# Three attention mixers: the value product with the probabilities as the stationary side

## The chip, the cores and the metric

The program runs on one core of a Trainium2 chip. The metric is the device time of one execution in microseconds. Five engines work side by side in that core: TensorE (PE, with its weight loads shown apart as PEld), VectorE (DVE), ScalarE (ACT), GpSimd (POOL) and SyncE (SP, which here only starts transfers).

## What is computed

Two blocks of two layers each run on 256 tokens of width 1024. In the first block, layer 0 mixes by a differential attention and a gated recurrence, layer 1 by dilated attention with 16 heads of 64. In the second block each layer holds a gated linear attention of 4 heads, a neighbourhood attention of 6 heads and a sliding-window attention of 6 heads with a sink, all of head width 64; its layer 0 also carries a context of 256 tokens through its own attention. Feed-forward layers stand between them. The attention that the change touches is this, in the reference:

```python
# dilated attention (block 1, layer 1), one branch
m = jnp.max(s, axis=-1, keepdims=True)
e = jnp.exp(s - m)
den = jnp.sum(e, axis=-1)
o = jnp.einsum('bhrnqk,bhrnkd->bhrnqd', e.astype(v.dtype), vw) / den[..., None].astype(v.dtype)
...
# sliding window with a sink (block 2)
p = jax.nn.softmax(jnp.concatenate([s_loc, s_ctx, s_sink], axis=-1), axis=-1)
...
o = (jnp.einsum('bhgnqk,bnkhd->bnqhgd', p_loc, vb)
     + jnp.einsum('bhgnqk,blhd->bnqhgd', p_ctx, vc))
```

The neighbourhood attention is the same without the sink and with a bias; the context's attention has its own 256 keys alone.

## The kernel before

**The dense work.** All weights come from HBM in units of 512 KB or less (`WeightStream`, lines 195 to 223). SP starts the transfer into `wr`, ACT rounds it to `wh` (line 214), DVE takes the rest `wl` (line 216), and each product of activations and weights is made of three matmuls, `xh*wh`, `xh*wl`, `xl*wh`, on operands of type fp32r that pass the array once. These matmuls, 256 or 512 columns wide, are most of PE's work.

**The small work** of the mixers (scores, transposes, value products) is in plain fp32. A plain fp32 matmul runs as two instructions in the profile, a transpose as one.

**One attention step** handles two heads (`c` = 0, 1) and one tile of 128 queries (`t`). It is a pipeline of three functions, `one`, `two` and `three`; at place i of the program `one` of step i, `two` of step i-1 and `three` of step i-2 are written down. `one` makes the scores and the softmax: maximum, exponential (ACT, which also adds up the sums), reciprocal, and then a DVE multiplication of each row of probabilities by its reciprocal (lines 751 and 1257). `two` transposes the probabilities on PE, 128 by 128 at a time, and copies them to SBUF. `three` is the value product (lines 774 and 1286): the values of a head (128 keys by 64) are the stationary operand, the transposed probabilities (128 keys by 128 queries) move, and the two heads go to output rows 0 to 63 and 64 to 127 of one PSUM tile. So the array works as two halves of 64 columns, written `128*64` in the profile, and the output has the feature on the rows and the token along the columns, as the output projection wants it. `y["T"].put` then splits it into high and low part (ACT line 357, DVE line 358).

There are 52 such steps: 16 in the dilated attention (8 with one key tile, 8 with two), 12 in the context's attention (two key tiles) and 24 in the latent attention of the two layers of block 2 (four key tiles). With two heads, so many key tiles and two instructions each, a step has 4, 8 or 16 value-product instructions, 576 in all.

**What sets the order.** The program is a list of items (`weave`, `side_by_side`) in which attention steps are woven into projections or feed-forward parts. A scheduler then orders each engine's instructions by a simulated timeline, so that the order on an engine isn't that of the code. PSUM has four buffers with the tag `acc`, two `sc`, one `sm`, one `fil`. The modulation (line 958) is a side job: its matmuls work on a quarter of the array's columns (`128*32`), with a stationary `cT` of 32 columns per step of which two carry data.

## Time and profile before

| | us |
|---|---|
| median of 3 runs | 1947.28 |
| lowest, highest | 1944.61, 1950.41 |
| the profiled execution's own time | 1951.42 |
| its span, first to last instruction | 1949.5 |
| PE busy | 1859.0 |
| weight loads (PEld) busy | 1582.9 |
| DVE busy | 1230.2 |
| ACT busy | 1006.3 |
| mean granted clock of TensorE | 0.967 |

Busy time is the union of an engine's instructions. Matmuls overlap each other, so how long PE takes over a stretch is read from the distance between the starts of its instructions, not from the durations. The granted clock is a share of 2.4 GHz.

### The profile page before, as it was taken

How to read it: one execution, taken by the hardware profiler on the slowest of the kernel's cores; microseconds unless marked ns; L12 is line 12 of the kernel's file. 1: busy time of each engine (PE TensorE's matmuls, PEld its weight loads, DVE VectorE, ACT ScalarE, POOL GpSimd, SP SyncE). 2: the span in 40 equal slices, each digit the busy share in tenths (PEclk: the TensorE clock that was granted, in tenths of full speed). 3: DMA queues.
4: the chain of work that ended last, by engine and by line, in shares of the span. 5: the costliest groups of instructions: out<-in, count | busy, mean ns of one | idle time of the engine just before them, and what ended most of it. 6: DMA issues, size and time to landing. Idle time of an engine off the chain costs nothing. (4 is left out here: it accounts for less than half of the span.)

```text
span 1949.5 us, 32053 instructions
## 1 busy us (share of the span) xinstructions
PE 1859.0 (95%) x12481; PEld 1582.9 (81%) x12481; DVE 1230.2 (63%) x2325; ACT 1006.3 (52%) x1669; POOL 168.0 (9%) x230
## 2 busy tenths in 40 slices
PE   8989999997999799999899999999999999979997
PEld 6766889886886588887697999989999986659997
DVE  5565566665666566667667786676646767655554
ACT  6354556444555355555456664454646556434443
POOL 3111300003110200002100000000000001100000
PEclk9999999997998889999899999999999999989999
DMA  8755654545666544446552445555664455346563
GB/s 294 245 173 195 200 192 152 184 145 185 194 217 196 175 154 153 161 155 214 165 184 90 125 149 161 177 186 180 190 188 154 143 184 171 122 151 176 185 181 106
DMA packets 101539, 338.87 MB, mean 174 GB/s; under 512 B 12212, under 2 KB 13516, under 8 KB 101388
## 3 DMA queue, kind: packets, MB, share of 16 engines
q1 hardware_dynamic: 86124, 286.00, 46.0%
q0 software_dynamic: 15264, 50.84, 7.9%
q8 instruction: 98, 1.61, 0.3%
q14 instruction: 53, 0.43, 0.1%
HBM read 335.73 MB, written 1.05 MB: 173 GB/s over the span
## 5 line engine op out<-in xcount | busy, mean ns | idle before, releaser
L216 DVE TENSOR_TENSOR wl<-wr,wh 128x1024 fp32r<-128x1024 f32 (+3 forms) x562 | 644.1, 1148 | 409.5 <-ACT wh L214 406.7
L214 ACT CAST wh<-wr 128x1024 fp32r<-128x1024 f32 (+3 forms) x562 | 549.3, 980 | 620.5 <-PE acc L281 129.1
L280 PE MATMUL acc<-wl,mh 128*128 128x256 f32 (+3 forms) x400 | 131.7, 330 | 1.5 <-DVE wl L216 1.5
L279 PE MATMUL acc<-wh,mh 128*128 128x256 f32 (+3 forms) x400 | 131.8, 336 | 0.0
L281 PE MATMUL acc<-wh,ml 128*128 128x256 f32 (+3 forms) x400 | 131.8, 331 | 0.0
L279 PE MATMUL acc<-wh,xh 128*128 128x512 f32 (+3 forms) x304 | 119.9, 401 | 2.6 <-ACT xh L378 1.9
L280 PE MATMUL acc<-wl,xh 128*128 128x512 f32 (+3 forms) x304 | 118.8, 391 | 0.5 <-DVE wl L216 0.5
L281 PE MATMUL acc<-wh,xl 128*128 128x512 f32 (+3 forms) x304 | 118.2, 390 | 0.0
L956 POOL DMA_DIRECT2D fr<-in_w_mod_dram x90 | 48.9, 545 | 661.9 <-PE fil L958 547.8
L854 PE MATMUL acc<-wh,a 128*128 128x512 f32 x256 | 101.5, 400 | 0.0
L856 PE MATMUL acc<-wh,a 128*128 128x512 f32 x256 | 101.1, 396 | 0.0
L855 PE MATMUL acc<-wl,a 128*128 128x512 f32 x256 | 101.1, 395 | 0.0
L1474 PE MATMUL sc<-xh,wh 128*128 128x256 f32 x352 | 100.4, 286 | 0.5 <-ACT xh L378 0.5
L1475 PE MATMUL sc<-xl,wh 128*128 128x256 f32 x352 | 100.7, 286 | 0.0
L1476 PE MATMUL sc<-xh,wl 128*128 128x256 f32 x352 | 100.2, 285 | 0.0
L1475 PE MATMUL sc<-ml,wh 128*128 128x256 f32 x352 | 98.9, 281 | 0.0
L1476 PE MATMUL sc<-mh,wl 128*128 128x256 f32 x352 | 98.7, 280 | 0.0
L1474 PE MATMUL sc<-mh,wh 128*128 128x256 f32 x352 | 98.7, 280 | 0.0
L958 PE MATMUL fil<-fr,cT 128*32 128x256 f32 x720 | 65.9, 422 | 31.2 <-DMA fr<-in_w_mod_dram 30.7
L279 PEld LDWEIGHTS acc<-wh,mh 128*128 128x128 f32 x400 | 75.2, 189 | 12.4 <-issue 4.8
L829 PE MATMUL sc<-mh,wh 128*128 128x256 f32 x256 | 74.1, 291 | 9.3 <-ACT mh L378 9.3
L280 PEld LDWEIGHTS acc<-wl,mh 128*128 128x128 f32 x400 | 75.9, 190 | 8.0 <-DVE wl L216 1.9
(580 smaller groups left out, 4853.5 us busy)
## 6 DMA issues: line engine op xcount, KB each, us to landing
wr<-in_ffn_w_dram SPq DMA_DIRECT2D x128, 512.0 KB, 3.4
fr<-in_w_mod_dram POOLq DMA_DIRECT2D x90, 512.0 KB, 5.0
wr<-in_w_gate_dram SPq DMA_DIRECT2D x66, 512.0 KB, 3.7
wr<-in_w_up_dram SPq DMA_DIRECT2D x66, 512.0 KB, 4.1
wr<-in_w_down_dram SPq DMA_DIRECT2D x66, 512.0 KB, 3.6
wr<-in_w_in_dram SPq DMA_DIRECT2D x40, 384.0 KB, 3.4
wr<-in_ev_w_in_dram SPq DMA_DIRECT2D x28, 512.0 KB, 5.4
wr<-in_w_in_dram SPq DMA_DIRECT2D x28, 512.0 KB, 3.9
```

Source lines behind the costliest of these rows:

```text
L214: S.copy(hi, raw)
L216: V.tensor_tensor(lo, raw, hi, ALU.subtract)
L279: mm(o, xh[:, k, :], wh[:, kk, :], start=(u == 0 and kk == 0), stop=False)
L280: mm(o, xh[:, k, :], wl[:, kk, :], start=False, stop=False)
L281: mm(o, xl[:, k, :], wh[:, kk, :], start=False, stop=(u == nu - 1 and kk == 1))
L829: mm(o, wh[:, kk, bs], mh, start=(k == 0 and b % 2 == 0), stop=False, skip_group_check=True)
L854: mm(o, hh[:, b, ts_], wh[:, kk, :], start=(b == 0), stop=False)
L855: mm(o, hh[:, b, ts_], wl[:, kk, :], start=False, stop=False)
L856: mm(o, hl[:, b, ts_], wh[:, kk, :], start=False, stop=(b == 3))
L1474: mm(o, wh[:, kk, bs], mh, start=(k == 0 and b == 0), stop=False, skip_group_check=True)
L1475: mm(o, wh[:, kk, bs], ml, start=False, stop=False, skip_group_check=True)
L1476: mm(o, wl[:, kk, bs], mh, start=False, stop=(k == 7), skip_group_check=True)
```

## The change

The roles in the value product are exchanged: in `heads_out` the transposed probabilities are stationary (all 128 columns of the array) and the 64 columns of values move. The output has tokens on the rows. It is multiplied by the reciprocal sums on its way out of PSUM into `yt` (DVE, line 729), transposed on PE into the other part of the same PSUM tile, and then split as before. The multiplications of the probabilities in `one` are gone. In the sliding window's latent part the sink becomes the start value of the first maximum, so that its own maximum goes. The remaining edits make room: `cT` shrinks to overlapping windows of 32 columns, and two small tags have three buffers in place of four. The differential attention (`da1`, `da2`, `da_out`) stays as it is.

```diff
-    cT = T([P, KD, 32], F32, "cT")
+    cT = T([P, 2 * KD + 30], F32, "cT")
...
-        v = T([P, n], F32, tag + "a", 4)
+        v = T([P, n], F32, tag + "a", 3)
...
+    def heads_out(y, blk, t, rr, pvs):
+
+        o = PT("acc")
+        for c, pairs in enumerate(pvs):
+            for j, (p, v) in enumerate(pairs):
+                mm(o[:, 64 * c:64 * c + 64], p, v, start=(j == 0), stop=(j == len(pairs) - 1))
+        yt = T([P, 2, 64], F32, "yt", 2)
+        V.tensor_tensor(yt, o[:, 0:P].rearrange("p (c n) -> p c n", c=2), rr.unsqueeze(2).to_broadcast([P, 2, 64]), ALU.mult)
+        tr(o[:, P:2 * P], yt.rearrange("p c n -> p (c n)"))
+        y["T"].put(blk, 1, t, o[:, P:2 * P].unsqueeze(1))
...
-            s, rr = softmax_pair(ps, C("odd")[:, 256 - nk:256], nk)
-            for c in range(2):
-                V.tensor_scalar(s[:, c, 0:nk], s[:, c, 0:nk], rr[:, c:c + 1], None, ALU.mult)
-            return (s,)
+            return softmax_pair(ps, C("odd")[:, 256 - nk:256], nk)
...
-            o = PT("acc")
-            for j in range(t + 1):
-                for c in range(2):
-                    hs = slice((2 * hp + c) * 64, (2 * hp + c) * 64 + 64)
-                    mm(o[64 * c:64 * c + 64, 0:P], v[:, j, hs], pT[:, c, j, :], start=(j == 0), stop=(j == t))
-            y["T"].put(4 * half + hp, 1, t, o[:, 0:P].unsqueeze(1))
+            heads_out(y, 4 * half + hp, t, rr,
+                      [[(pT[:, c, j, :], v[:, j, (2 * hp + c) * 64:(2 * hp + c) * 64 + 64]) for j in range(t + 1)]
+                       for c in range(2)])
...
-                mm(ps[32 * g:32 * g + 32, 0:256], cT[:, k, :], raw[:, 256 * g:256 * g + 256],
+                mm(ps[32 * g:32 * g + 32, 0:256], cT[:, 2 * k:2 * k + 32], raw[:, 256 * g:256 * g + 256],
...
-                                           ALU.max, mx[:, 1, c:c + 1])
+                    V.tensor_tensor_reduce(s[c][:, 256:W], ps[c][:, 256:W], zero.to_broadcast([P, 256]), 1.0,
+                                           -3.0e38 if na else sink[:, c:c + 1], ALU.add, ALU.max, mx[:, 1, c:c + 1])
...
-            if not na:
+            if e.ctx and not na:
                 V.tensor_tensor(m, m, sink, ALU.max)
...
-            for c in range(2):
-                V.tensor_scalar(s[c], s[c], sm[:, 0, c:c + 1], None, ALU.mult)
-            return (s,)
+            return s, sm[:, 0, :]
...
+            heads_out(y, 2 + hp, t, rr, [[(pTs[c][:, j * P:(j + 1) * P], value(c, j)) for j in range(nkt)] for c in range(2)])
```

**What moves, place by place.** In the rows below a name stands as output<-moving,stationary, a number at its end is the buffer's, and a plain fp32 matmul is one row although it runs as two instructions. First PE at the last step of block 2's layer 0, in the middle of the context's feed-forward (lines 1553 to 1555). Before:

```order
L1554 MATMUL acc_11854<-xl_10495,wh_11702 128x256
L1555 MATMUL acc_11854<-xh_10494,wl_11704 128x256
L1286 MATMUL acc_11879<-fr_11676,sv_9892 64x128 x4
L1286 MATMUL acc_11879<-fr_11676,csv_4409 64x128 x4
L1553 MATMUL acc_11854<-xh_10494,wh_11708 128x256
L1554 MATMUL acc_11854<-xl_10495,wh_11708 128x256
```

The value product of both heads stands among the dense matmuls, 64 output rows by 128 columns each. Now, at the same step:

```order
L1554 MATMUL acc_11885<-xl_10526,wh_11733 128x256
L1555 MATMUL acc_11885<-xh_10525,wl_11735 128x256
L727 MATMUL acc_11910<-sv_9918,fr_11704 128x64 x2
L727 MATMUL acc_11910<-csv_4409,fr_11704 128x64 x2
L727 MATMUL acc_11910<-sv_9918,fr_11704 128x64 x2
L727 MATMUL acc_11910<-csv_4409,fr_11704 128x64 x2
L1553 MATMUL acc_11885<-xh_10525,wh_11739 128x256
L1554 MATMUL acc_11885<-xl_10526,wh_11739 128x256
```

The product is again eight matmuls in a row, with 128 output rows by 64 columns and the probabilities (`fr`) as stationary side; the transpose of `yt` stands 27 matmuls further on.

Next PE at the end of the dilated attention (block 1, layer 1; `a_1210` are the values, `t_...` the probabilities). Before:

```order
L279 MATMUL acc_6405<-wh_6247,xh_4768 128x512
L280 MATMUL acc_6405<-wl_6249,xh_4768 128x512
L774 MATMUL acc_6453<-t_1339_6437,a_1210_5914 64x128 x2
L281 MATMUL acc_6405<-wh_6247,xl_4769 128x512
L774 MATMUL acc_6458<-t_1342_6451,a_1210_5914 64x128 x4
L279 MATMUL acc_6404<-wh_6247,xh_4768 128x512
L280 MATMUL acc_6404<-wl_6249,xh_4768 128x512
L281 MATMUL acc_6404<-wh_6247,xl_4769 128x512
```

The two last value products stand close together among the dense matmuls, and there is no transpose after them. Now, for the same end of the stage:

```order
L727 MATMUL acc_6446<-a_1217_5917,t_1337_6397 128x64 x4
L177 MATMUL acc_6456<-ident_61,t_1347_6431 128x128 x4
L279 MATMUL acc_6413<-wh_6252,xh_4768 128x512
L280 MATMUL acc_6413<-wl_6254,xh_4768 128x512
L281 MATMUL acc_6413<-wh_6252,xl_4769 128x512
L963 MATMUL fil_6815<-fr_6888,cT_72 32x256 x3
L963 MATMUL fil_6815<-fr_6894,cT_72 32x256 x4
L727 MATMUL acc_6463<-a_1217_5917,t_1352_6444 128x64 x2
L177 MATMUL acc_6446<-ident_61,yt_6451 128x128
L177 MATMUL acc_6463<-ident_61,yt_6466 128x128
L279 MATMUL acc_6414<-wh_6252,xh_4768 128x512
L280 MATMUL acc_6414<-wl_6254,xh_4768 128x512
```

Between the second last product (acc_6463) and the transpose of its quotient only one other transpose stands; the product before it (acc_6446) has sixteen between, seven of them modulation (line 963).

Last DVE at that same end of the dilated attention. Before:

```order
L494 RECIPROCAL rs_6430<-sm__1336_6424 128x2
L751 TENSOR_SCALAR t_1334_6422<-t_1334_6422,rs_6430 128x256 x2
L216 TENSOR_TENSOR wl_6402<-wr_6398,wh_6400 128x1024
L216 TENSOR_TENSOR wl_6469<-wr_6465,wh_6467 128x1024
L358 TENSOR_TENSOR xl_4769<-acc_6439,xh_4768 128x128
L216 TENSOR_TENSOR wl_6487<-wr_6483,wh_6485 128x1024
L358 TENSOR_TENSOR xl_4769<-acc_6453,xh_4768 128x128
```

The probabilities are multiplied (line 751) right behind the reciprocal, and only the low parts of the finished outputs (line 358) follow the weight splits (line 216). Now:

```order
L494 RECIPROCAL rs_6439<-sm__1349_6433 128x2
L216 TENSOR_TENSOR wl_6485<-wr_6481,wh_6483 128x1024
L216 TENSOR_TENSOR wl_6503<-wr_6499,wh_6501 128x1024
L729 TENSOR_TENSOR yt_6451<-acc_6446,rs_6361 128x128
L729 TENSOR_TENSOR yt_6466<-acc_6463,rs_6390 128x128
L358 TENSOR_TENSOR xl_4769<-acc_6446,xh_4768 128x128
L358 TENSOR_TENSOR xl_4769<-acc_6463,xh_4768 128x128
L729 TENSOR_TENSOR yt_6476<-acc_6471,rs_6439 128x128
```

The two multiplications of the probabilities are gone, and the two divisions of the outputs (line 729) stand behind two weight splits and ahead of the low parts.

## Rows read from the trace of the kernel before

**Rows 1.** The page: busy time, and PE in 40 slices (tenths busy).

```profile
PE 1859.0 (95%) x12481; PEld 1582.9 (81%) x12481; DVE 1230.2 (63%) x2325; ACT 1006.3 (52%) x1669; POOL 168.0 (9%) x230
...
PE   8989999997999799999899999999999999979997
```

**Rows 2.** Busy time of each engine in the four attention stretches.

```profile
core 0: us, PE busy (x) PEld busy (x) DVE busy (x) ACT busy (x) POOL busy (x), PEclk, DMA share, GB/s
540.00:652.00 112.00, 107.53 (x823) 82.61 (x816) 67.81 (x267) 59.00 (x156) 10.65 (x20) 0.94 0.63 201
700.00:873.00 173.00, 173.00 (x1159) 148.48 (x1159) 118.68 (x211) 99.75 (x182) 2.01 (x2) 1.00 0.51 167
1005.00:1190.00 185.00, 179.61 (x1350) 156.45 (x1349) 138.89 (x342) 118.50 (x204) 6.70 (x12) 0.99 0.43 138
1600.00:1705.00 105.00, 98.30 (x804) 71.72 (x803) 71.90 (x237) 51.94 (x119) 15.02 (x26) 0.94 0.46 146
```

**Rows 3.** What PE waited for in the whole span: total, times, longest, us.

```profile
PE fil L958 <- DMA fr<-in_w_mod_dram: 30.7, 19, 7.5
...
PE sm L177 <- DVE t L1257: 3.8, 2, 2.5
```

**Rows 4.** PE in order of time, latent layer 0, around one value product.

```profile
start us, us, engine line op out<-in xcount [idle before <-releaser]
...
1184.57 0.28 PE L1555 MATMUL acc<-xh,wl 128*128 128x256 f32 x1
1184.78 0.66 PE L1286 MATMUL acc<-fr,sv 128*64 128x128 f32 x8
1185.27 0.61 PE L1286 MATMUL acc<-fr,csv 128*64 128x128 f32 x8
1185.81 0.39 PE L1553 MATMUL acc<-xh,wh 128*128 128x256 f32 x1
1186.03 0.28 PE L1554 MATMUL acc<-xl,wh 128*128 128x256 f32 x1
```

**Rows 5.** PE, the gated mixer's output products, full-array form.

```profile
1176.27 0.28 PE L1555 MATMUL fil<-xh,wl 128*128 128x256 f32 x1
1176.39 1.90 PE L1152 MATMUL acc<-a,t 128*128 128x64 f32 x16
1178.21 0.27 PE L1161 MATMUL acc<-cf,t 64*64 64x64 f32 x1
```

**Rows 6.** PE, transposes: a row of them, and two between 512-wide matmuls.

```profile
1091.13 0.60 PE L177 MATMUL acc<-ident,t 128*128 128x128 f32 x4
...
639.45 0.39 PE L281 MATMUL acc<-wh,xl 128*128 128x512 f32 x1
639.69 0.38 PE L177 MATMUL acc<-ident,t 128*128 128x128 f32 x2
639.82 0.48 PE L279 MATMUL acc<-wh,xh 128*128 128x512 f32 x1
640.13 0.40 PE L280 MATMUL acc<-wl,xh 128*128 128x512 f32 x1
```

**Rows 7.** DVE by line: busy us, mean ns, idle before.

```profile
L216 DVE TENSOR_TENSOR wl<-wr,wh 128x1024 fp32r<-128x1024 f32 (+3 forms) x562 | 644.1, 1148 | 409.5 <-ACT wh L214 406.7
...
L1257 DVE TENSOR_SCALAR t<-t,sm 128x512 f32<-128x512 f32 x48 | 21.1, 482 | 0.5
...
L751 DVE TENSOR_SCALAR t<-t,rs 128x128 f32<-128x128 f32 (+1 forms) x32 | 8.7, 313 | 0.5
...
L1257 DVE TENSOR_SCALAR t<-t,csm 128x256 f32<-128x256 f32 x24 | 7.4, 350 | 0.4
...
L1170 DVE TENSOR_TENSOR t<-acc,g4stb 128x128 f32<-128x128 f32 x8 | 2.0, 286 | 4.4 <-POOL g4stb L385 4.3
...
L1247 DVE TENSOR_TENSOR mx<-mx,sink__56_234 128x2 f32<-128x2 f32 x6 | 0.9, 155 | 0.0
```

More of the change, by code (lines that the diff above doesn't have):

```diff
@@ L193, in params @@
         V.tensor_copy(prm.rearrange("p a l k -> p (a l k)"), pt[:, 0:96])
-        S.activation(cT[:, :, 0:2].rearrange("p k s -> p s k"), pt[:, 96:112].rearrange("p (s k) -> p s k", s=2), AF.Silu)
+        S.activation(cT[:, 0:2 * KD].rearrange("p (k s) -> p s k", s=2), pt[:, 96:112].rearrange("p (s k) -> p s k", s=2), AF.Silu)
     def PR(name, l):
@@ L381, in rsqrt_eps @@
     def rsqrt_eps(ms, n, eps, tag="st"):
-        v = T([P, n], F32, tag + "a", 4)
+        v = T([P, n], F32, tag + "a", 3)
         V.tensor_scalar(v, ms, eps, None, ALU.add)
-        r = T([P, n], F32, tag + "b", 4)
+        r = T([P, n], F32, tag + "b", 3)
         nc.gpsimd.tensor_tensor(r, v, mhalf[:, 0:n], ALU.pow)
@@ L748, in one, with two @@
                 mm(ps[c][:, 0:nk], q[r, hp, t * P:(t + 1) * P], k[r, hp, 0:nk], start=True, stop=True)
-            s, rr = softmax_pair(ps, C("odd")[:, 256 - nk:256], nk)
-            for c in range(2):
-                V.tensor_scalar(s[:, c, 0:nk], s[:, c, 0:nk], rr[:, c:c + 1], None, ALU.mult)
-            return (s,)
-        def two(half, hp, t, s):
+            return softmax_pair(ps, C("odd")[:, 256 - nk:256], nk)
+        def two(half, hp, t, s, rr):
             nk = P * (t + 1)
@@ L765, in two, with three @@
                 S.copy(pT, p4)
-            return (pT,)
-        def three(half, hp, t, pT):
+            return pT, rr
+        def three(half, hp, t, pT, rr):
             v = st["v", half]
-            o = PT("acc")
-            for j in range(t + 1):
-                for c in range(2):
-                    hs = slice((2 * hp + c) * 64, (2 * hp + c) * 64 + 64)
-                    mm(o[64 * c:64 * c + 64, 0:P], v[:, j, hs], pT[:, c, j, :], start=(j == 0), stop=(j == t))
-            y["T"].put(4 * half + hp, 1, t, o[:, 0:P].unsqueeze(1))
+            heads_out(y, 4 * half + hp, t, rr,
+                      [[(pT[:, c, j, :], v[:, j, (2 * hp + c) * 64:(2 * hp + c) * 64 + 64]) for j in range(t + 1)]
+                       for c in range(2)])
         def group(half, j0, t_outer=()):
@@ L1239, in one @@
                 else:
-                    V.tensor_tensor_reduce(s[c][:, 256:W], ps[c][:, 256:W], zero.to_broadcast([P, 256]), 1.0, -3.0e38, ALU.add,
-                                           ALU.max, mx[:, 1, c:c + 1])
+                    V.tensor_tensor_reduce(s[c][:, 256:W], ps[c][:, 256:W], zero.to_broadcast([P, 256]), 1.0,
+                                           -3.0e38 if na else sink[:, c:c + 1], ALU.add, ALU.max, mx[:, 1, c:c + 1])
                     nb = nbt[0][:, c, t, :] if na else (C("causal") if t == 0 else C("swa"))
@@ L1255, in one, with two @@
             V.reciprocal(sm[:, 0, :], sm[:, 0, :])
-            for c in range(2):
-                V.tensor_scalar(s[c], s[c], sm[:, 0, c:c + 1], None, ALU.mult)
-            return (s,)
-        def two(hp, t, s):
+            return s, sm[:, 0, :]
+        def two(hp, t, s, rr):
             if e.ctx or hp < 3:
@@ L1273, in two, with three, value @@
                     V.tensor_copy(pTs[c], pt[:, 0:W])
-            return (pTs,)
-        def three(hp, t, pTs):
-            o = PT("acc")
-            for j in range(nkt):
+            return pTs, rr
+        def three(hp, t, pTs, rr):
+            def value(c, j):
                 src = e if j < 2 else ctxkv
-                for c in range(2):
-                    if hp < 3:
-                        vv = src.nv[:, j % 2, (2 * hp + c) * 64:(2 * hp + c + 1) * 64]
-                    else:
-                        kv = (2 * hp - 6 + c) // 3
-                        vv = src.sv[:, j % 2, kv * 64:(kv + 1) * 64]
-                    mm(o[64 * c:64 * c + 64, 0:P], vv, pTs[c][:, j * P:(j + 1) * P], start=(j == 0), stop=(j == nkt - 1))
-            y["T"].put(2 + hp, 1, t, o[:, 0:P].unsqueeze(1))
+                if hp < 3:
+                    return src.nv[:, j % 2, (2 * hp + c) * 64:(2 * hp + c + 1) * 64]
+                kv = (2 * hp - 6 + c) // 3
+                return src.sv[:, j % 2, kv * 64:(kv + 1) * 64]
+            heads_out(y, 2 + hp, t, rr, [[(pTs[c][:, j * P:(j + 1) * P], value(c, j)) for j in range(nkt)] for c in range(2)])
         return pipeline([(hp, t) for hp in hps for t in range(2)], one, two, three)
```

## The prediction

> **What bounds the kernel now.** I read the page first. PE is busy for 95% of the span, DVE for 63%, and in 33 of the 40 slices PE stands at nine tenths or more [rows 1]. Then I read the same by stretch, for the four in which the changed steps run: the dilated attention (540 to 652 us), the context's attention (700 to 873), and the latent attention of block 2's layer 0 (1005 to 1190) and layer 1 (1600 to 1705). PE is busy for 558 of these 575 us, DVE for 397 [rows 2]. Third, what PE waited for: its longest wait in total is for the modulation's weights, 30.7 us; for the multiplied probabilities it waited 3.8 us in all, in two places [rows 3]. So in these stretches the order of PE's instructions, taken one after the other, sets the pace, and DVE is hidden. Last I read PE in order of time around single products, from start to start, since a union of durations hides what an instruction really costs there.
>
> **The price of one product instruction.** In the old form 16 instructions start between 1184.78 and the next dense matmul at 1185.81; the first eight last 0.66 us to the end of the last, and with 0.27 us for one they start (0.66 - 0.27)/7 = 0.055 us apart [rows 4]. The new form is in the trace already: the gated mixer's output product has a full 128-column stationary side and 64 moving columns. Sixteen of them last 1.90 us, so they start (1.90 - 0.27)/15 = 0.109 us apart [rows 5]. Transposes, with 128 stationary and 128 moving columns, start (0.60 - 0.27)/3 = 0.110 us apart [rows 6]. Halving the moving columns changes nothing there, and halving the stationary ones halves the price: loading the stationary side sets it. The exchange doubles the stationary columns of each instruction, from 64 to 128. With 576 product instructions that is 576 x (0.109 - 0.055) = **+31.1 us**.
>
> The Trainium skill's TensorEngine Tiling (Array Packing), section Performance Considerations, advises the opposite of the change: where the moving side has 64 columns or fewer, swap the two sides and tile by columns, for up to 2x. By that alone the products' 31.7 us would become 63.4 us. The rows agree on the factor of two, but the advice leaves out the next term, which works against it.
>
> **What the half arrays cost at their borders.** Before the group the distance from the last dense start to the first product is 0.21 us (1184.57 to 1184.78), where dense matmuls of 256 columns stand 0.12 apart: +0.09. Behind it, 16 x 0.055 = 0.88 us of the 1.03 us up to the next dense start are the group's own: +0.15. The dense matmul after that stands 0.22 behind instead of 0.12: +0.10 [rows 4]. Together 0.34 us a visit, or 0.17 for each change of the array's tiling. The new form shows none on entering: 1176.27 to 1176.39 is the usual 0.12 [rows 5]. Along PE's whole order I count 467 changes of tiling before and 400 now; some 110 go with the products and some come back, because modulation (`128*32`) and scores (`64*128`) are cut up more often. 67 x 0.17 = **-11.4 us**. How the new form leaves for dense matmuls no row shows; the nearest are transposes, after which two dense matmuls follow with nothing lost (below), so I take nothing. The other end is 0.34 us for each of 52 steps, +17.7 us, if all of a visit's price returned.
>
> **The 52 transposes.** Two transposes between 512-wide matmuls: from 639.45 to 640.13 is 0.68 us with one dense matmul in between, and two dense distances of 0.23 would be 0.46, so 0.11 us each [rows 6]. 52 x 0.11 = **+5.7 us**.
>
> **DVE.** It loses 48 x 0.482 + 24 x 0.350 + 32 x 0.313 = 41.5 us of multiplications, and 12 maxima of 0.155 us, 1.9 us. It gains 52 divisions of 128 x 128 out of PSUM; the gated mixer's division is the same form, 0.286 us, so 14.9 us [rows 7]. Net 28.5 us less, beside PE and so worth only what PE waited for it. Of the 3.8 us for the probabilities I take 3 back [rows 3]: **-3 us**; bounds 0 and -7, if the other DVE waits of these stretches go too.
>
> **The new wait.** Each step now goes from PE to DVE and back to PE. The scheduler puts work between: in the latent step shown, 27 dense matmuls, some 3.5 us at 0.12 and 0.23; the median step has about 3 us. In seven of the 52 I count less than 1.3 us between, four of them in the dilated attention, the nearest having one transpose between. One round is a matmul's 0.27 us and a division's 0.286 us and what is ahead of it on DVE, in the worst case a weight split of 1.148 us [rows 7], so 0.6 to 1.7 us against a mean cover of 0.8. I take 0.4 us for seven: **+3 us**; bounds 0 and, with a split ahead in a dozen places, +12. Behind a waiting transpose stand dense matmuls on PE; behind a waiting division stand weight splits on DVE, which PE then needs.
>
> **Edits at nothing.** The memset of `cT` shrinks at the start, where PE waits for other things. The smaller `cT` gives the modulation the same 32 stationary columns. Two tags with three buffers instead of four: their tiles are a few columns and POOL, which fills them, is busy 9% [rows 1]; if that cover is gone one step of the norms comes late, under 1 us. The sink as a start value costs DVE at most the 0.155 us a step that it saves.
>
> **The sum.** 31.1 - 11.4 + 5.7 - 3 + 3 = 25.4 us. PE's own waits in these stretches, for modulation weights above all, end at a fixed time, so some added work falls into them: PE isn't busy for 17 of 575 us [rows 2], and I take 4 us of that. 21.4 us against the profiled execution: its span of 1949.5 us and 1.9 us around it, 1951.4, becomes 1973. That execution stands 4.1 us above the median of the runs shown, 1947.3, to which the forecast refers: 1947.3 + 21.4 = **1969 us**.
>
> **Rivals.**
> *The stationary load hides and the moving columns count (faster).* The queue would load the next 128 columns while others move, and an instruction of 64 moving columns would cost no more than one of 128 does now, 0.055 us. Then the +31.1 us fall away and 25.4 becomes -5.7 us, 1942; at half of 0.055 another 576 x 0.027 = 15.8 us go, 1926. It decides below 0.065 us an instruction. Against it: the same form at 0.109 us, with nothing ahead of it that it waits for [rows 5]. In the Trainium skill's TensorE: Matmul & The Clock Gate, section Back-to-back issue gap, the table gives 134 cycles for 128 columns and about 60 for 64 at 2.4 GHz, which by itself makes the exchange a gain; the same section says that the load counts too. Chance 0.05.
> *PE's waits and DVE take it in (no change).* If the stretches wait for the softmax chain rather than for PE, the 28.5 us taken from DVE shorten that chain and the added PE work falls into waits. All 17 us of idle PE would have to be used, and the 7 us of DVE waits gone: 28.4 - 17 - 7 = 4 us, 1952. For it: 15 of the 17 us lie where steps are dense on DVE. Against: the context's stretch has no idle PE at all, and much of the idle time elsewhere is the modulation's transfers [rows 2, 3]. Chance 0.09.
> *The round over DVE decides (much slower).* If a division always stood behind a split, and its transpose at the head of PE's queue, each step would lose up to 1.7 us less its cover. It decides where the round takes over 3 us; 26 steps at 1 us make 26 us, 1995. Against: the cover in the order, and that DVE has less to do. Chance 0.05.
> *The borders stay (slower still than forecast).* The new form might pay on leaving what the old one paid: +17.7, 1987. Chance 0.08.
>
> **How the numbers follow.** The forecast has 0.73. Its own range is 1958 to 1980, from the bounds of the small terms. Taken with the neighbours on either side, **1953 to 1985** leaves out the fast rival, most of the much slower one and part of the border. About 0.3%, 5.8 us, is what a measurement of this kernel can tell from no change. Faster by more than that: the first rival and a sliver of lucky order, 0.06. Within: the second, 0.09. Slower: 0.85.
>
> **What would show it.** Right: line 727 with 576 instructions of the form `128*128 128x64`, starting 0.109 us apart and entered at 0.12; 52 transposes of `yt`; DVE's busy time some 28 us lower; the four stretches longer, the two latent ones most (24 x 16 of the 576 instructions); dense matmuls following a product at once. Wrong: product instructions near 0.055 us apart; PE waiting for `yt` from DVE by more than 10 us; the stretches as long as before with PE idle less; or a change outside of the four stretches as large as in them.

## The result

The changed kernel takes 1977.13 us in the median (1973.19 to 1982.53, 4 runs), the kernel before in the same series 1948.85 (4 runs). The ratio is 1.0134, with a 95% interval of 1.0107 to 1.0161: some 26 us slower, where 1969 us and +21.4 had been forecast. The profiled execution took 1978.46 us, with a span of 1976.7.

The page of the profile after, which answers to [rows 1]:

```profile
PE 1891.9 (96%) x12533; PEld 1623.7 (82%) x12533; DVE 1199.8 (61%) x2261; ACT 1003.9 (51%) x1669; POOL 170.8 (9%) x230
```

PE has 32.9 us more, DVE 30.4 less. The value product in the latent step of layer 0, in order of time, answers to [rows 4]:

```profile
1202.09 0.28 PE L1555 MATMUL acc<-xh,wl 128*128 128x256 f32 x1
1202.21 0.56 PE L727 MATMUL acc<-sv,fr 128*128 128x64 f32 x4
1202.60 0.61 PE L727 MATMUL acc<-csv,fr 128*128 128x64 f32 x4
1203.05 0.61 PE L727 MATMUL acc<-sv,fr 128*128 128x64 f32 x4
1203.49 0.61 PE L727 MATMUL acc<-csv,fr 128*128 128x64 f32 x4
1203.91 0.36 PE L1553 MATMUL acc<-xh,wh 128*128 128x256 f32 x1
1204.12 0.28 PE L1554 MATMUL acc<-xl,wh 128*128 128x256 f32 x1
```

The group is entered at the usual 0.12 us, and its 16 instructions take 1203.91 - 1202.21 = 1.70 us up to the next dense start, 0.106 us each. The dense matmul behind it stands 0.21 away in place of 0.12, so leaving costs 0.09. One visit takes 1.79 us, where the old form with its borders took 0.09 + 1.03 + 0.10 = 1.22 [rows 4].

The transpose of the quotient between two 512-wide dense matmuls (it answers to [rows 6]), and the division on DVE in the latent steps with its count, shortest, median and longest time in ns (it answers to [rows 7]):

```profile
1207.34 0.39 PE L1581 MATMUL acc<-wh,c 128*128 128x512 f32 x1
1207.57 0.27 PE L177 MATMUL acc<-ident,yt 128*128 128x128 f32 x1
1207.60 0.47 PE L1579 MATMUL acc<-wh,c 128*128 128x512 f32 x1
1207.91 0.39 PE L1580 MATMUL acc<-wl,c 128*128 128x512 f32 x1
```

```profile
L729 DVE TENSOR_TENSOR yt<-acc,sm x24: 278/285/294, 1034.4 to 1729.1; 128x128 f32<-128x128 f32 x24
```

From the dense matmul ahead of the transpose to the next but one is 1207.91 - 1207.34 = 0.57 us; less two dense distances of 0.23 that leaves 0.11. What PE waited for in the changed kernel, total, times and longest in us (the form of [rows 3]):

```profile
PE sc L834 <- ACT mh L378: 1.0, 1, 1.0
...
PE acc L177 <- DVE yt L729: 0.3, 1, 0.3
```

The new wait, PE for the quotient, is 0.3 us in the whole execution; for the modulation's weights PE waited 35.4 us, in before 30.7 [rows 3].

**Where the 27.2 us of the span went.** The 562 weight splits (line 216) come in the same order in both traces, so the start of one of them, after less before, tells how far behind the changed kernel is there. Cut at the same splits, the stretches that differ are these; first before (columns as in [rows 2]), then after:

```profile
core 0: us, PE busy (x) PEld busy (x) DVE busy (x) ACT busy (x) POOL busy (x), PEclk, DMA share, GB/s
0.00:162.90 162.90, 148.70 (x843) 107.38 (x844) 94.63 (x233) 84.70 (x166) 34.92 (x65) 0.97 0.68 227
548.30:660.10 111.80, 107.33 (x790) 80.75 (x788) 67.62 (x250) 57.71 (x147) 9.86 (x19) 0.94 0.59 187
660.10:704.80 44.70, 29.44 (x160) 23.59 (x160) 25.89 (x42) 18.34 (x37) 14.49 (x17) 0.73 0.41 145
704.80:899.70 194.90, 194.90 (x1275) 166.14 (x1274) 129.82 (x222) 106.73 (x186) 2.09 (x2) 1.00 0.53 174
899.70:1255.80 356.10, 344.37 (x2374) 297.94 (x2373) 252.71 (x504) 199.81 (x324) 28.80 (x32) 0.98 0.49 154
1589.20:1754.00 164.80, 145.49 (x1062) 108.43 (x1062) 106.31 (x311) 77.36 (x163) 19.74 (x34) 0.91 0.47 151
```

```profile
0.00:171.40 171.40, 155.89 (x843) 112.51 (x844) 93.68 (x233) 83.93 (x166) 34.89 (x65) 0.91 0.65 218
556.90:678.10 121.20, 116.79 (x821) 91.58 (x820) 63.46 (x235) 56.13 (x147) 10.68 (x20) 0.94 0.55 174
678.10:713.70 35.60, 27.77 (x153) 21.89 (x152) 20.30 (x41) 18.10 (x37) 15.58 (x15) 0.76 0.48 179
713.70:912.40 198.70, 197.90 (x1280) 172.18 (x1280) 124.65 (x213) 106.11 (x186) 2.09 (x2) 1.00 0.52 170
912.40:1274.00 361.60, 352.29 (x2385) 310.36 (x2384) 246.16 (x485) 199.63 (x324) 29.79 (x32) 0.98 0.48 152
1607.20:1781.20 174.00, 155.64 (x1074) 118.78 (x1073) 99.14 (x293) 78.27 (x164) 19.55 (x34) 0.92 0.44 143
```

A stretch's length has three parts that these rows give: PE idle (length less PE busy), what the clock took, estimated as length times (1 - granted clock), and the rest, which I call PE's work at full clock. (PEclk has two places, so the clock's part is good to half a hundredth of the length, 0.6 to 1.8 us in the four stretches. And where PE stands still at the lower clock, that time counts in both of the first two parts, so the rest comes out too low. Counted from the traces' clock with PE's busy time alone, the work below grows by 9.3, 2.9, 7.9 and 12.3 us in the four attention stretches, 32.4 together, in place of 8.9, 3.0, 7.8 and 11.1.)

| stretch | length, us | PE idle | taken by the clock | PE's work | forecast for the work |
|---|---|---|---|---|---|
| up to the diff. attention | +8.5 | +1.3 | +10.5 | -3.3 | 0 |
| dilated attention | +9.4 | -0.1 | +0.6 | +8.9 | 5.2 + 1.8 - 1.7 = 5.3 |
| border behind it | -9.1 | -7.4 | -3.5 | +1.9 | 0 |
| context's attention | +3.8 | +0.8 | 0 | +3.0 | 5.2 + 1.3 - 3.7 = 2.8 |
| latent, layer 0 | +5.5 | -2.4 | +0.1 | +7.8 | 10.4 + 1.3 - 4.3 = 7.4 |
| latent, layer 1 | +9.2 | -1.0 | -0.9 | +11.1 | 10.4 + 1.3 - 0.2 = 11.5 |

The last column is the prediction's three terms, by stretch: 96, 96, 192 and 192 instructions at 0.054 us; 16, 12, 12 and 12 transposes at 0.11; and the changes of tiling counted in the traces, which go from 86 to 76, 54 to 32, 85 to 60 and 82 to 81, at 0.17. In the four stretches the work is 30.8 us more, the forecast by stretch 27.0; only the dilated attention is off by more than the clock's rounding. Two things were not forecast at all, +8.5 and -9.1 us in places outside the attention that the exchange touches. That they cancel is luck: nothing in the record ties the one to the other.

### The profile page after: what moved, and what is told of

It is laid out like the page before. It is cut to its first block, busy times and chain, and to the rows that moved or that the text cites. A ratio compares the mean times of both kernels' runs of the same rounds, so it can differ in the third digit from the quotient of the medians.

```text
span 1976.7 us, 32088 instructions
## 1 busy us (share of the span) xinstructions
PE 1891.9 (96%) x12533; PEld 1623.7 (82%) x12533; DVE 1199.8 (61%) x2261; ACT 1003.9 (51%) x1669; POOL 170.8 (9%) x230
## 5 line engine op out<-in xcount | busy, mean ns | idle before, releaser
L963 PE MATMUL fil<-fr,cT 128*32 128x256 f32 x720 | 72.6, 430 | 36.8 <-DMA fr<-in_w_mod_dram 35.4
L1474 PE MATMUL sc<-mh,wh 128*128 128x256 f32 x352 | 98.6, 280 | 0.0
L281 PEld LDWEIGHTS acc<-wh,ml 128*128 128x128 f32 x400 | 75.8, 189 | 6.7 <-DVE ml L358 0.4
```

The costliest lines, as they stand in the source:

```text
L281: mm(o, xl[:, k, :], wh[:, kk, :], start=False, stop=(u == nu - 1 and kk == 1))
L963: mm(ps[32 * g:32 * g + 32, 0:256], cT[:, 2 * k:2 * k + 32], raw[:, 256 * g:256 * g + 256], start=(k == 0), stop=(k == KD - 1), tile_posit ...
L1474: mm(o, wh[:, kk, bs], mh, start=(k == 0 and b == 0), stop=False, skip_group_check=True)
```

## The experiments

**The edits apart.** Three kernels between before and after.

```diff
# e1: before, with this alone (and the two lines that fill and read cT)
-    cT = T([P, KD, 32], F32, "cT")
+    cT = T([P, 2 * KD + 30], F32, "cT")
...
# e2: after, with the old cT; to make room, yt has 1 buffer and the small tags 2
-    cT = T([P, 2 * KD + 30], F32, "cT")
+    cT = T([P, KD, 32], F32, "cT")
...
# e8: before, with these alone (the other small tag likewise)
-        v = T([P, n], F32, tag + "a", 4)
+        v = T([P, n], F32, tag + "a", 3)
...
-  ... 1.0, -3.0e38, ALU.add,
+  ... 1.0, -3.0e38 if na else sink[:, c:c + 1], ALU.add,
...
-            if not na:
+            if e.ctx and not na:
```

> The kernel before with the edit of cT alone (46 columns and overlapping windows in place of 256 columns; the result is the same). Its instruction order is that of the changed kernel, row for row, up to the dilated attention. Theory: the scheduler's other order in block 1's layer 0, caused by this edit, holds some 8 of the change's 27 us (the lead of the weight splits grows by 8.5 us between 141 and 163 us of the trace). Then +8 us against before, 1957, from that stretch. Rival: all of the change's time lies in the exchange itself and the early shift is a difference between two executions: 0 us, 1949. A wait of DVE on POOL near 676 us, which the changed kernel doesn't have, may go as well and take up to 9 us back: then the trace shows the +8 before 200 us and less at the end.

Measured 1957.54 us, ratio 1.0031 (1.0009 to 1.0053): about 6 us slower by itself. Its trace is 7.4 us behind before at the weight split that starts at 191 us there, and 2.9 at the end; the execution traced was one of its shorter ones (1954.36 us). So the edit that I had costed at nothing makes most of the +8.5.

> The changed kernel with cT as before (256 columns); to fit, yt has one buffer and the two small tags two. Its order is that of before up to the dilated attention. Theory: the early 8 us are gone, 1977 - 8 = 1969, +20 against before, at 200 us no shift. Rival that the exchange holds all: 1977. One buffer of yt could cost some us more, shown as waits for yt.

Measured 1968.43 us, ratio 1.0084 (1.0060 to 1.0108), as expected. At 191 us it is 0.2 us ahead of before: the early loss is gone with the edit. In layer 1 it loses 16.4 us, of which only 10.7 are work (table below); the clock takes 6.9 more than in before.

> The kernel before with the two edits that make room beside cT: the sink as start value, and three buffers for the two small tags. The order is that of before up to block 2's layer 0. Theory: nothing, 1949 +- 3. Rival, these edits hold part of the time: +6 us or more.

Measured 1949.50 us, ratio 0.9989 (0.9972 to 1.0007): the buffers and the sink's start value are worth nothing that can be measured, as costed.

**The price of one product instruction.** In e3 the kernel before takes a stationary side of 128 columns without the exchange; in e6 the changed kernel moves 32 columns in place of 64.

```diff
# e3 (the latent step; the dilated one likewise)
-                    mm(o[64 * c:64 * c + 64, 0:P], vv, pTs[c][:, j * P:(j + 1) * P], ...)
+                    mm(o[:, c * P:(c + 1) * P], src.sv[:, j % 2, 0:P], pTs[c][:, j * P:(j + 1) * P], ...)
# e6
-                mm(o[:, 64 * c:64 * c + 64], p, v, start=(j == 0), stop=(j == len(pairs) - 1))
+                mm(o[:, 64 * c:64 * c + 32], p, v[:, 0:32], start=(j == 0), stop=(j == len(pairs) - 1))
```

> The kernel before, probabilities multiplied as before and no transposes of outputs, but the stationary side of the value product is the 128 columns of two heads instead of 64, one product into its own 128 columns of PSUM per head, of which half the rows are used (in two of the three pairs of sliding-window heads one head so takes the other group's values). It leaves out the exchange and keeps its two terms: twice the stationary columns and no half arrays. Theory: 576 x 0.054 = +31.1 us and 385 - 467 = 82 changes of tiling fewer at 0.17, -13.9 us: +17 us, 1966. Rival, that the exchange costs by transposes and the round over DVE: near 0 us, 1949 or below, since those are not in this kernel.

Measured 1970.53 us, ratio 1.0099 (1.0077 to 1.0121), +19 us with no exchange, no division and no transposes: giving each product the whole array, with the changes of tiling that this saves, is most of the loss. (ACT and DVE split the outputs in 104 pieces here in place of 52.)

> The changed kernel with 32 of the 64 moving columns in each value product (both halves of a head's output get the same 32 values; the division is two instructions of half the width). Theory, the stationary load sets the price: starts stay 0.109 us apart and the time that of the changed kernel, 1977 +- 4. Rival, the moving columns set it: 576 x 0.027 us = 15.6 us less, 1961.

Measured 1984.07 us, ratio 1.0164 (1.0139 to 1.0190), no less than the changed kernel and 3 us above the range expected. (Its trace has a DVE subtraction of 7.2 us at the border, told of below, that the changed kernel's doesn't have.) The group at the same step, in order of time:

```profile
1204.50 0.53 PE L727 MATMUL acc<-sv,fr 128*128 128x32 f32 x4
1204.87 0.61 PE L727 MATMUL acc<-csv,fr 128*128 128x32 f32 x4
1205.32 0.61 PE L727 MATMUL acc<-sv,fr 128*128 128x32 f32 x4
1205.76 0.61 PE L727 MATMUL acc<-csv,fr 128*128 128x32 f32 x4
1206.21 0.36 PE L1555 MATMUL acc<-xh,wh 128*128 128x256 f32 x1
```

1206.21 - 1204.50 = 1.71 us for 16, as with twice the moving columns (1.70). So the rival in which the moving columns count is out.

That the number of stationary columns sets the price doesn't follow, and the trace of before speaks against it. Two places of the dilated attention, in order of time: a step with one key tile, both heads in a row, and a product of one head that stands alone, on one half of the array:

```profile
557.97 0.44 PE L774 MATMUL acc<-t,a 128*64 128x128 f32 x4
575.56 0.43 PE L774 MATMUL acc<-t,a 128*64 128x128 f32 x2
```

The four instructions of two heads take no longer than the two of one head. Instruction by instruction, 552 of the 576 start in pairs, one of each head, some 0.007 us apart, and the pairs follow each other every 0.11 us (0.16 the first time). Instructions on one half alone also start 0.109 us apart, with 64 stationary columns as others with 128. So the 0.055 us of the prediction is the mean of two half arrays that work at the same time, and what the change gives up is that, not a cheaper load. What sets the 0.11 us is not shown.

**The round over DVE.** e4 is the changed kernel without it.

```diff
-        yt = T([P, 2, 64], F32, "yt", 2)
-        V.tensor_tensor(yt, o[:, 0:P].rearrange("p (c n) -> p c n", c=2), rr.unsqueeze(2).to_broadcast([P, 2, 64]), ALU.mult)
-        tr(o[:, P:2 * P], yt.rearrange("p c n -> p (c n)"))
-        y["T"].put(blk, 1, t, o[:, P:2 * P].unsqueeze(1))
+        y["T"].put(blk, 1, t, o[:, 0:P].unsqueeze(1))
```

> The changed kernel without the division and the transpose of the output (52 divisions and 52 transposes left out; the undivided output goes on as it stands, tokens on the rows). Theory: 52 x 0.11 = 5.7 us and 368 - 400 = 32 changes of tiling at 0.17, 5.4 us less than the changed kernel, which is 26 us above before: +15 us, 1964. If the wait of DVE on POOL near 680 us is in this kernel, some 7 us more, 1971; the trace shows it. Rival, that the round from PE over DVE and back is what the exchange costs: less than 1955.

Measured 1966.95 us, ratio 1.0088 (1.0063 to 1.0113). The round is worth some 9 us (0.0046 of 1952; each of the two ratios is known to about 5 us), against 5.7 for the transposes and 3 for the wait in the forecast. Since PE waited for the quotient 0.3 us in all, it should be PE's own work, and the traces bear this out (below). The wait of DVE on POOL that the expectation allows for is in this trace at half its length, 4.35 us.

**What the multiplications cost.** e5 is the kernel before without them.

```diff
-            for c in range(2):
-                V.tensor_scalar(s[c], s[c], sm[:, 0, c:c + 1], None, ALU.mult)
# and the same two lines of the dilated attention
```

> The kernel before without the multiplication of the probabilities by the reciprocal sums (left out; the outputs stay undivided). Theory: DVE is hidden behind PE, and the 41.5 us of DVE work are worth 0 to 7 us: 1946 (1941 to 1950). Rival, DVE's work sets the attention stretches: 15 us or more, 1935 or below.

Measured 1931.05 us, ratio 0.9903 (0.9880 to 0.9926), -19 us. My expectation missed by 15; the rival had the time. Cut as above, layer 1's latent stretch is:

```profile
1585.50:1734.00 148.50, 137.08 (x1053) 100.79 (x1052) 96.18 (x285) 77.36 (x164) 20.57 (x34) 0.98 0.50 167
```

Layer 1 is 16.2 us shorter than in before: 7.9 of it less idle PE, and 14.8 - 3.0 = 11.8 less taken by the clock, with 3.5 more of work (by busy time alone 9.6 less and 1.2 more). The other stretches make up the rest with both signs (the border 8.6 shorter, the context's attention behind it 6.3 longer). But what PE waited for in layer 1 is above all the modulation's weights, in before and then in e5:

```profile
PE fil L958 <- DMA fr<-in_w_mod_dram: 14.2, 8, 7.5
PE fil L956 <- DMA fr<-in_w_mod_dram: 9.0, 9, 3.6
```

So PE's list of waits for the probabilities, 3.8 us, is far from all that leaving the multiplications out is worth, and the time that the clock takes is in no row of that list. How much of the 19 us is DVE's work itself, and how much an order that meets these transfers better, is not shown. The same three parts of layer 1's stretch in every kernel whose stretch tells something, cut at the same splits:

| kernel | length, us | PE idle | taken by the clock | PE's work |
|---|---|---|---|---|
| before | 164.8 | 19.3 | 14.8 | 130.7 |
| e8, tags and sink | 158.5 | 18.0 | 9.5 | 131.0 |
| e7, norm on DVE | 170.7 | 21.2 | 18.8 | 130.7 |
| e9, split | 158.9 | 17.6 | 9.5 | 131.8 |
| e14, split and norm | 153.6 | 15.9 | 6.1 | 131.6 |
| e5, no multiplication | 148.6 | 11.4 | 3.0 | 134.2 |
| e4, no round | 169.2 | 15.6 | 16.9 | 136.7 |
| e3, wide load | 167.9 | 15.7 | 11.8 | 140.4 |
| after | 173.9 | 18.4 | 13.9 | 141.6 |
| e2, after with the old cT | 181.2 | 18.1 | 21.7 | 141.4 |

The work falls into levels: 131 to 134 with the old product, 140 to 142 with the whole array (137 without the round), and these 10 us are what the edit of the product does here. By busy time alone the levels are 133 to 135 and 142 to 145 (139). The lengths scatter over 33 us, because idle time and clock scatter. Each row is one execution, and e8, whose median is that of before, is 6.3 us shorter here: a difference of that size in this stretch doesn't show what caused it.

**The 9 us at the border.** In before, DVE and POOL behind the dilated attention, in order of time:

```profile
675.61 9.49 DVE L379 TENSOR_TENSOR ml<-t,mh 128x512 fp32r<-128x512 f32 x2
```

```profile
674.13 2.51 POOL L407 TENSOR_TENSOR x<-x,bc 128x512 f32<-128x512 f32 x2
676.60 1.26 POOL L408 TENSOR_TENSOR x<-x,bc 128x512 f32<-128x512 f32 x1
677.82 2.47 POOL L407 TENSOR_TENSOR x<-x,bc 128x512 f32<-128x512 f32 x2
680.26 3.69 POOL L408 TENSOR_TENSOR x<-x,bc 128x512 f32<-128x512 f32 x3
```

One subtraction of 128 x 512 lasts from 675.61 until POOL's row of eight without a gap ends at 683.95, and a little on; PE waits 9.3 us for what follows it, where the changed kernel waited 1.0 (line 834 in its rows above):

```profile
PE sc L829 <- ACT mh L378: 9.3, 1, 9.3
```

The durations of line 379 over the whole execution (shortest, median, longest in ns), before and then after:

```profile
L379 DVE TENSOR_TENSOR ml<-t,mh x20: 675/684/8891, 118.8 to 1556.2; 128x512 fp32r<-128x512 f32 x20
```

```profile
L379 DVE TENSOR_TENSOR ml<-t,mh x20: 669/690/1767, 117.0 to 1574.4; 128x512 fp32r<-128x512 f32 x20
```

8.89 us against a median of 0.68 before, and after at most 1.77. In e1 and e3 the long one is there, 8.9 and 8.5 us, in e6 7.2, in e4 and e5 4.35; in e2 it isn't. What decides it, presumably what starts just ahead of what, was not tried.

The Trainium skill's SBUF — State Buffer, section SBUF: two separate sides, says that an operation of DVE with two inputs in SBUF and one of GpSimd that reads SBUF take a shared pair of ports for a whole instruction, and that the other then blocks. The rows agree, and show more: blocked by one instruction of 1.25 us the subtraction would have lasted about 1.9 us, as the 1.77 after; here DVE did not get its turn between the seven of them that were still to end. e7 moves these eight operations of POOL to DVE (POOL has 222 instructions in place of 230):

```diff
-            nc.gpsimd.tensor_tensor(x[t][:, cs], x[t][:, cs], st["g"][:, cs], ALU.mult)
-            nc.gpsimd.tensor_tensor(x[t][:, cs], x[t][:, cs], st["b"][:, cs], ALU.add)
+            eng = V if (l, n) == (1, "ln1") else nc.gpsimd
+            eng.tensor_tensor(x[t][:, cs], x[t][:, cs], st["g"][:, cs], ALU.mult)
+            eng.tensor_tensor(x[t][:, cs], x[t][:, cs], st["b"][:, cs], ALU.add)
```

> The kernel before with the gain and bias of one layer norm (block 1, layer 1, the one behind the dilated attention; 8 operations of lines 407 and 408) on DVE instead of POOL. Theory: one DVE subtraction of line 379 there takes 8.9 us instead of 0.7 because POOL's eight operations run beside it without a gap, and PE waits 9.3 us for it; without them the 8.9 us go, at the price of 8 x 0.69 us of DVE work beside PE: -7 us, 1943. Rival, the wait is set by something else (the norm's own chain, the weights): the same time as before, 1950, and PE still waits 9 us for line 378.

Measured 1948.11 us, ratio 0.9981 (0.9957 to 1.0004). The long subtraction is gone, PE's wait for line 378 there falls from 9.3 to 0.6 us, and the border is 7.8 us shorter in the trace. The next stretch is 2.0 longer, and layer 1's 5.9, 4.0 of it by the clock (table). So the collision is the cause at the border; over the whole, this edit alone can't be told from no change.

**The 8 us at the start.** The stretch from 140 us on (columns as in [rows 2]), first before to 150 us, then after to 155:

```profile
140.00:145.00 5.00, 3.60 (x38) 2.48 (x39) 4.15 (x12) 1.09 (x4) 0.95 (x2) 1.00 0.98 370
145.00:150.00 5.00, 3.72 (x34) 2.63 (x33) 2.09 (x8) 0.59 (x1) 0.63 (x2) 1.00 0.53 181
```

```profile
140.00:145.00 5.00, 2.63 (x18) 1.82 (x20) 0.00 (x0) 0.03 (x1) 0.53 (x1) 0.59 0.75 292
145.00:150.00 5.00, 4.33 (x23) 3.38 (x21) 3.36 (x12) 0.58 (x1) 0.00 (x0) 0.50 0.34 105
150.00:155.00 5.00, 4.48 (x23) 3.05 (x23) 0.82 (x2) 0.00 (x0) 0.00 (x0) 0.50 0.00 0
```

In the changed kernel the granted clock is at its lower level, 1.2 GHz, for some 20 us. What PE did before it fell, and the same 16 score instructions at the two levels (after; then before):

```profile
142.37 1.08 PE L963 MATMUL fil<-fr,cT 128*32 128x256 f32 x8 [4.43 <-DMA fr<-in_w_mod_dram]
143.38 3.09 PE L623 MATMUL sc<-a,t 64*128 64x128 f32 x16
```

```profile
141.97 1.71 PE L623 MATMUL sc<-a,t 64*128 64x128 f32 x16
```

PE waited 4.43 us for a tile of modulation weights (in before 1.54), and what came next took 3.09 us in place of 1.71. The four kernels with the small cT and nothing in that wait (e1, e4, e6, after) all have the lower level for 20.5 us there. Those with the old cT have it between 140 and 165 us for nothing (before, e9) up to 10 us: in e5, after a wait of 2.5 us, for 10.2, and e5 is 4.6 us behind before at 191 us, e8 4.4. So some loss there comes without the edit of cT too. Two kernels put useless work into that wait: 20 matmuls of zeros, added into the open sum, on the kernel with the small cT alone (e12) and on the changed kernel (e13).

```diff
                 nc.gpsimd.dma_start(raw, A["w_mod_2"][l, k * P:(k + 1) * P, j * D:(j + 1) * D])
+                if early[0] == 20:
+                    for _ in range(20):
+                        mm(ps[:, 0:P], zero.to_broadcast([P, P]), ident, start=False, stop=False)
```

> The kernel before with the small cT (as in the cT edit alone, which measured 1957.5 us, +6.0) and 20 full-array fp32 matmuls of zeros by the identity, added into the open sum of the modulation, which change nothing in the result. On PE they stand just before the matmuls of the 20th modulation weight tile, where the cT edit alone waited 4.3 us for that tile and where the granted clock was 0.5 from 140 to 160 us. They are 40 instructions of 0.110 us, 4.4 us of useless work. Theory of the clock: the cT edit costs its 6 to 8 us because PE stands still there and the clock is then granted at half; with PE at work during the wait the rows from 140 to 160 us stay at 1.00, the weight splits from 165 us on lie 6 to 8 us earlier than with the cT edit alone, and the median is about 1951, that is no change against before. Rival, the order: the changed order of PE's instructions there is itself the longer one; then the useless work hides in the wait at best, the splits stay where they were, 1957, or come later by what doesn't hide, up to 1961.

Measured 1953.40 us, ratio 0.9997 (0.9981 to 1.0013): no change against before, where the cT edit alone was 6 us slower. The useless work, the scores and the wait that is left:

```profile
135.58 4.73 PE L959 MATMUL fil<-ident,zero 128*128 128x128 f32 x40
...
141.03 1.16 PE L623 MATMUL sc<-a,t 64*128 64x128 f32 x16
...
144.70 0.91 PE L961 MATMUL fil<-fr,cT 128*32 128x256 f32 x8 [2.15 <-DMA fr<-in_w_mod_dram]
```

The scores take 1.16 us, the granted clock is 0.67 from 145 to 150 us and 0.99 or more in the rest of 140 to 160, and the weight split at 191 us is 1.3 us ahead of before, where the cT edit alone was 7.4 behind. 40 instructions that change nothing in the result won back 8.7 us up to there, so the wait with the lower clock behind it was the loss. Of the 8.7 us 4.0 go again at once: PE waits 5.6 us for weight splits (1.6 with the cT edit alone), and at 254 us of before's trace the two are 1.8 and 6.5 us behind it. The order of PE's instructions behind the filler changed a little with it; that the filler alone did it is therefore not quite clean, but no work was taken away.

> The changed kernel (1977.1 us) with the same 20 matmuls of zeros before the 20th modulation weight tile, where it waited 4.4 us. Theory of the clock: the low stretch of 140 to 160 us goes, the splits from 165 us on lie some 8 us earlier than in the changed kernel, and the median is about 1969. Rival, the order: 1977 to 1981.

Measured 1974.83 us, ratio 1.0117 (1.0090 to 1.0143), against 1.0134 for the changed kernel: some 3 us less, which isn't clear of noise, where 8 had been expected. At 191 us the trace is 10.5 us ahead of the changed kernel; then PE waits 6.1 us for weight splits (1.6 in the changed kernel), which leaves 4.0 us of lead at 254, and at the border the collision is back with a subtraction of 7.2 us. Winning time in one place moved the others.

**A version that beats both.** The multiplications shared between DVE and ACT (e9; the lines of the dilated attention likewise), and that with e7's edit (e14).

```diff
             for c in range(2):
-                V.tensor_scalar(s[c], s[c], sm[:, 0, c:c + 1], None, ALU.mult)
+                if c == 0:
+                    V.tensor_scalar(s[c], s[c], sm[:, 0, c:c + 1], None, ALU.mult)
+                else:
+                    S.activation(s[c], s[c], AF.Copy, scale=sm[:, 0, c:c + 1])
```

> The kernel before with one of the two multiplications of the probabilities on ACT (a scaled copy) and the other left on DVE, so that the two run side by side; nothing else is changed. DVE loses 20.7 us of work, ACT gains about 52 of some 0.5 us, 27 us. Leaving the multiplications out altogether gave -18.9 us, of which the shift of the weight splits puts 16 us into block 2's layer 1 (1589 to 1754 us), where PE stood still less and the granted clock stayed at 1.00. Theory: that gain comes from the shorter chain through DVE in that layer; half of the chain's saving stays, the layer is 5 to 10 us shorter, and the median is 1940 to 1946. Rival: what ends these waits is the arrival of the modulation's weights, and the gain without the multiplications was the luck of an order that met them; then no change, 1948 to 1954. Second rival: ACT is late with the rounding of weights, slower than 1954.

Measured 1945.11 us, ratio 0.9961 (0.9943 to 0.9979), the time that the first theory had. ACT's copies of 128 x 512 take 0.72 us; layer 1 is 5.9 us shorter, 5.3 of it by the clock. The theory's reason is not shown by it: PE waits 14.2 us for the modulation's weights in this layer as in before, and e8, with both multiplications on DVE, has the layer as short (table).

> The kernel before with both edits that measured shorter by themselves: one multiplication of each pair on ACT (1945.1 us, -7.0) and the 16 multiplications and additions of the norm in block 1's layer 1 on DVE in place of POOL (1948.1, -3.7). They act in different places, the one in block 2's layer 1, the other at the border behind the dilated attention. If they add up: 1952 - 7.0 - 3.7 = 1941. Rival: what is won at the border is waited for again further on, where PE needs weights that arrive at their own pace; then 1945, as with the split alone.

Measured 1933.74 us, ratio 0.9924 (0.9896 to 0.9953), by the ratios some 15 us faster than before and 41 faster than the changed kernel. (The norm's edit moves eight operations, as in e7, not sixteen.) The two edits' ratios multiplied give 0.9942, inside this interval: that they do more together than apart isn't clear of noise. Layer 1's stretch is 11.2 us shorter than in before (table), with nearly the same work: idle PE 3.4 less, the clock 8.7 less. Why the norm's edit lengthens this stretch by itself and not together with the split stays open; PE's wait for the modulation's weights there is 16.9 us in e7 and 8.7 in e14 (14.2 in before), and no run took that alone.

## Why the prediction was right

*The load of the stationary side, +31.1.* The size was right, the reason was not. The new form measured 0.106 us an instruction against 0.109, and e3 shows the loss without the exchange. But "loading the stationary side sets it" was read from two rows that differ in a second thing: in the old form two heads worked on two halves of the array at once. An instruction with 64 stationary columns on one half alone costs 0.109 us too. The factor of two came out because 552 of the 576 instructions had a partner on the other half. (The division (0.66 - 0.27)/7 is 0.0557 rather than 0.055, so the term is some 30.5; nothing hangs on it.)

*The borders, -11.4, and none on leaving.* The sum is right where it can be checked by stretch: the context's attention, where 22 of 54 changes go, got only 3.0 us of work for its 96 instructions, and layer 1, where one goes, 11.1. That nothing is paid on leaving was wrong: 0.09 us where a dense matmul follows at once. In the trace that is so behind 30 of the 57 groups in which the 576 instructions stand, each time with much the same distance (0.20 us to the next dense matmul in place of 0.12, or 0.32 in place of 0.23 where they are 512 wide), 2.7 us in all. The shorter group (0.106 for 0.109) gives 576 x 0.003 = 1.7 of it back. The 1.0 that remains is little of the gap between 25.4 and 30.8 us (32.4 by busy time alone); most of that gap stays open, and 3.6 of it lie in the dilated attention.

*The transposes, +5.7, and the wait, +3.* The transpose measured 0.11 as read before. The wait didn't come: PE stood 0.3 us for the quotient, as the order had covered it. The round without a wait still measured about 9 us; by the traces' work in the four stretches e4 has 19.8 us more than before, after 30.8, so 11.0. That is the 5.7 for the transposes and 32 more changes of tiling (368 in e4, 400 after), 5.4, which my count over the whole order had inside the border term.

*DVE, -3.* The step that failed in its reasoning, beside the first. I priced DVE's relief by PE's list of waits, 3.8 us, with 7 as the bound; leaving the multiplications out of the kernel before measured 19, most of it in layer 1 by a shorter wait for the modulation's weights and by the clock, neither of which that list puts down to DVE. That the multiplications themselves cost this much is not shown. In the changed kernel the relief was not seen: in layer 1 idle PE and the clock are together 1.9 us lower. Which of the new order's waits stand in its place was not tried.

*Edits at nothing.* Wrong for cT: +6 alone, by a wait of 4.3 us and the clock after it. Right for the tags and the sink.

*What PE's waits absorb, -4.* The idle time and the clock of the four stretches changed by -2.9 us together, close to it, though the clock was not in my reason, and this term, the relief of DVE and the wait that didn't come can't be told apart in it.

So the direction, the place and the size of the main terms were right, and the sum within the range: 25.4 us of work forecast on PE, 30.8 measured. The reason given for the largest term was wrong; its size was right because both prices were read from groups like those that the change exchanges. The named sign of error "a change outside of the four stretches as large as in them" came in part: +8.5 and -9.1, each nearly as large as the largest stretch. With one sign they would have put the forecast off by another 17 us, for reasons that it doesn't name; that they cancelled was luck.

## What to carry to other kernels

Before you widen a small matmul, ask what else the array does at the same time: here two products on two halves of it took no longer than one, and giving each the whole array paid for both. Then count the changes of tiling, which pay part of it back. On a kernel whose PE is busy 95% of the time, look at the granted clock beside the waits: a wait of 4 us was followed by 20 us at the lower clock, which cost more than the wait itself. And compare two traces at matching instructions rather than at equal times, since places that the change never touches can move by as much as the change itself.

## What the runs showed of the hardware

- A wait of PE can be paid twice: waits of 4.3 and 4.4 us at about 140 us were followed by some 20 us at a granted clock of 0.50, in which the same work took nearly double; in before a wait of 1.54 us at the same place was not. The Trainium skill's TensorE: Matmul & The Clock Gate, section HAM oscillation — how this bites in real kernels, tells of kernels whose matmuls wait for transfers between bursts and fall back to the lower clock; the rows agree. In runs of one and the same kernel time and clock go together too: of 18 runs of before, the shortest, 1945.75 us, had a mean granted clock of 0.971, the longest, 1959.96 us, 0.966.
- A row of POOL operations without a gap can hold one DVE operation for all of them: 8.89 us in place of 0.68.
- Two plain fp32 matmuls on two halves of the array (128 x 64 each) start some 0.007 us apart, and the four instructions of both take 0.44 us, where the two of one alone take 0.43.
- With a stationary side that changes every time, plain fp32 instructions on the whole array start on average 0.106 to 0.110 us apart with 32, 64 or 128 moving columns.
